# A decoder layer on one core: small products side by side, and another split of the counts in the top-k search

## The chip, the core and the metric

The kernel runs on one core of one Trainium2 chip. TensorE (PE in the rows) multiplies matrices on an array of 128 by 128 and writes to PSUM; VectorE (DVE), ScalarE (ACT) and GpSimd (POOL) work element by element or on small tables; SyncE (SP), ACT and POOL issue DMA transfers. Each engine executes its own queue in a fixed order and waits for others at semaphores. The metric is the device time of one execution in microseconds (us), lower is better.

## What is computed

One layer of a hybrid decoder, for 512 tokens of a prompt and for 8 samples of 4 new tokens with a paged cache of 4096 past tokens each. The width is 1024; everything is float32.

```
x = x + 1/2 * SwiGLU_1(rmsnorm(x))                    # hidden width 2816
gb, gc, hc, q, k, v, qi, ki, wi = split(rmsnorm(x) @ w_in)
y_conv = gb * causal_conv3(gc * hc)                   # 512 channels
I[t, s] = sum_h wi[t, h] * relu(qi[t, h] . ki[s])     # 8 indexer heads of 64
keys = top_k(I over the admissible keys)              # 128 for the prompt, 256 for a sample
attn = softmax(q . k[keys] / 8) @ v[keys]             # 8 heads of 64, 2 key groups
x = x + concat(y_conv, attn) @ w_out
x = x + 1/2 * SwiGLU_2(rmsnorm(x))
```

The new keys, values, indexer keys and convolution states are outputs too.

## The kernel before

The activations stay in SBUF, channels on the partitions, 544 tokens (32 of the samples, 512 of the prompt) in the free dimension. Weights come as float32 through a staging tile `wst` (as many as `WB` of them), and are split in two float32r parts, `whi` by ACT and the rest `wlo` by VectorE or POOL; each product is three matmuls on the parts. The program runs the first feed-forward part, the mixer, and the second feed-forward part.

The mixer is cut in steps that a planner (`PLAN`, `PLAN2`, `LAG`) interleaves; the order of each engine's queue then comes from a scheduler with priorities, at build time. What matters for the change:

- `sample_scores`: for the samples, pages of indexer keys are gathered (`kn`), transposed (`KTp`, then `kt` in SBUF), multiplied with the queries of two samples (`ssc`, two column groups of 64), passed through a relu (`Srel`), and summed over heads (`SC`, four column groups of 32).
- `sample_select`: the exact 256 best of 4100 scores of each query, found by three searches with two bits per round: 8 rounds on the high 16 bits of the score, 8 on the low 16, 7 on the position. A round tests three candidates: it counts the elements at or above each (`flip,cnt`), sums the counts of a query's four partitions by two small transposes (`row`, `col`), compares with the number needed, and forms the next candidates (`cand`). Two counts are VectorE's (L829), one is ACT's with the sign function (L827). The result is `bias`: 0 or a large negative number for each key.
- `prompt_select`: the top 128 of each prompt query, on VectorE, 16 pairs of maximum and replace on `pw` (L941, L942) for each of three blocks.
- `qk`: logits of a quarter of the pages for four samples: four gathers `ckn` by POOL, four `KTp` and `KT` (as many as `KTB` tiles), and eight matmuls `lg`, two for each sample, on the sample's column group of 32. Set 0's raw logits run during the search; set 1's run in `sample_attend`.
- `sample_attend`: adds `bias` to set 0's logits (`lgb`), takes the softmax, then four cycles of values of set 0 (four gathers `cvn`, a transpose `PT`, 32 matmuls `O`) and logits of set 1, then set 1's softmax and four groups of values. Keys and values share four gather buffers. `OT` ends a set.
- `prompt_softmax`: four logits `plg` for each block and head pair, each in a PSUM unit of one bank (`f`, two of them), evicted by VectorE with the mask added. `KTp`, `lg`, `lgb`, `PT` use large units of two banks (`w`, two of them).
- `conv` and `w_out` (`Yo`): matmuls that the planner places between these steps; the second half of `w_out` needs the samples' and the prompt's attention.

In the names of rows, `flip` is also the scratch that the counts write to, and `main` holds constants. A matmul on float32 operands leaves two records.

Of the kernel before, what the change touches and what calls it, by code (L numbers as in the profile page):

```python
# [46 lines left out]
WB = 3  # L47
# [9 lines left out]
LGD = 2  # L57
KTB = 3
# [8 lines left out]
def host_consts():  # L67
# [21 lines left out]
    need = np.where(p % 32 == 2, 2.0 * K_S - 4.0 * SCW, K_S)  # L89
    quarter = 4.0 ** np.arange(8)  # L90
    offs = np.stack([quarter, 2 * quarter, 0.5 - 3 * quarter], axis=1).reshape(1, 24)
    search = np.concatenate([need[:, None], np.broadcast_to([1.0, 1.0, -1.0], (128, 3)), np.broadcast_to(offs, (128, 24))], axis=1)
# [25 lines left out]
class Trunk:  # L118
# [14 lines left out]
    def tp(self, *args):  # L133
        ins = self.nc.tensor.transpose(*args)  # L134
        return self.tc.keep_in_program_order(ins) if self.pin else ins

# [18 lines left out]
    def stream(self, srcs, n, m, kind="", slot=None):  # L155
        """fp32 weights [128, n, m] from DRAM, as the two float32r parts, in the given or the next place of three."""
# [37 lines left out]
    def fmm(self, name, parts, act, n):  # L194
        """two PSUM banks, one per half of the tokens: W^T act over n k-tiles."""
# [35 lines left out]
    def rms(self, ssq):  # L231
        """sums of squares [128 tokens, 5 tiles] -> rn, 1 / root mean square."""
# [19 lines left out]
    def spread(self):  # L252
        """R [128, T]: the row of rn on every partition."""
# [9 lines left out]
    def ffn(self, wg, wu, wd, done, late=False):  # L263
# [3 lines left out]
        def hidden(f, G, U):  # L267
            """G, U: one PSUM tile of equal halves, or (columns, PSUM) pairs."""
# [95 lines left out]
    def begin_units(self):  # L364
        """loads and transposes the activations; the first gate and up units, by halves of the tokens as these come in."""
        nc, tc, i = self.nc, self.tc, self.i
        with tc.tile_pool(name="init", bufs=1) as ip, tc.high_priority(offset=FIRST):
# [13 lines left out]
            def weights(w, n):  # L381
                """w's first 128 columns in n runs of k-tiles: for each a function that loads it, fp32 and the two parts."""
# [57 lines left out]
            def mms(unit, w, hf, order="01234567" * 2):  # L440
                """the high parts of the weights at a k-tile's first mention, the low ones at its second."""
# [112 lines left out]
    def rope(self, v, i, n, nh, kind):  # L554
        """partial rotary on v [n tokens, nh, 64] of token tile i."""
# [32 lines left out]
    def load_half(self, pieces, m, ks=(4, 4), slots=(0, 1)):  # L588
        """w_in columns in runs of ks k-tiles, [128, k, m] each; pieces: (offset in tile, first column, width)."""
# [8 lines left out]
    def later(self, f, depth):  # L598
        """keep f for later; run what lies deeper than depth."""
# [5 lines left out]
    def idx_group(self, g, i, parts, depth=0):  # L605
        """steps; four indexer query heads of token tile i, and for g = 1 the indexer keys and head weights."""
# [45 lines left out]
    def qkv_group(self, g, i, parts, depth=0):  # L652
        """steps; four query heads of token tile i (g: 0, 1), or its keys and values (g: 2)."""
# [45 lines left out]
    def key_transpose(self, kn, name):  # L699
        """eight 128 x 128 transposes of gathered keys, PSUM -> SBUF."""  # L700
# [8 lines left out]
    def sample_scores(self, mp):  # L709
        """indexer scores of the sample queries over all pages: [128 = (bp, jh, b2, rr, t), (jl, p)]."""  # L710
# [20 lines left out]
        def headsum(out, S, bp, jh):  # L731
            self.mm(out, wm[:, bp, jh, :], S, start=True, stop=True)
# [10 lines left out]
        def scores(n):  # L743
            bp = n % 4
            w = self.wunit("ssc")
            for hf in range(2):
                for b2 in range(2):
                    self.mm(w[64 * b2:64 * b2 + 64, hf, :], self.qbi[:, 2 * bp + b2].rearrange("p r t h -> p (r t h)"),
                            kts[n, b2][:, hf * 512:(hf + 1) * 512], start=True, stop=True)
# [4 lines left out]
        def gathered(jh, c):  # L754
            u = self.tunit("SC")
            for bp in range(4):
                headsum(u[32 * bp:32 * bp + 32, :], SS[bp][:, c * 512:(c + 1) * 512], bp, jh)
# [43 lines left out]
    def sample_select(self, mp):  # L801
        """exact top K_S of the 4100 scores of each query (ties: lowest position first) -> bias 0 / -BIG."""
# [16 lines left out]
        def search(src, bits, base0):  # L819
            """[128, 1]: the largest x of base0 to base0 + 2**bits - 1 with K_S elements of the query at or above x,  # L820
            two bits a round: three candidates, counted on the vector engine (two) and the scalar engine."""
            base = mp.tile([128, 1], F32, name="base", tag="base", bufs=3)
            V.memset(base, base0)
            cand = mp.tile([128, 3], F32, name="cand", tag="cand", bufs=2)
            V.scalar_tensor_tensor(cand, self.sgn, base, self.offs[:, bits // 2 - 1], op0=ALU.mult, op1=ALU.add)
            for b in range(bits // 2 - 1, -1, -1):
                nc.scalar.activation(junk2, src, AF.Sign, bias=cand[:, 2:3], accum_out=cnt[:, 2:3])  # L827
                for k in range(2):
                    V.tensor_scalar(junk, src, cand[:, k:k + 1], None, op0=ALU.is_ge, op1=ALU.add, accum_out=cnt[:, k:k + 1])  # L829
                row = mp.tile([128, 32], F32, name="row", tag="row", bufs=2)  # L830
                V.transpose(row, cnt)
                if b:
                    nxt = mp.tile([128, 3], F32, name="nxt", tag="nxt", bufs=2)
                    V.scalar_tensor_tensor(nxt, self.sgn, base, self.offs[:, b - 1], op0=ALU.mult, op1=ALU.add)
# [11 lines left out]
                old, base = base, mp.tile([128, 1], F32, name="base", tag="base", bufs=3)  # L846
                V.tensor_add(base, old, add)
                yield
            return base
# [54 lines left out]
    def prompt_scores(self, pool):  # L904
        """indexer scores of prompt blocks 1..3, causally filled; block 0 keeps every admissible key."""
# [27 lines left out]
    def prompt_select(self, pool, scores):  # L933
        """the top K_P of the scores of each query (ties: lowest position first) -> 0 / -BIG."""
# [13 lines left out]
    def conv(self, cs, pool, early=False):  # L948
        """steps; the gated convolution of the channel chunks cs."""
# [73 lines left out]
    def qk(self, st, q, more):  # L1023
        """PSUM: raw logits of quarter q of the pages, samples 4 st to 4 st + 3; rows (b, g, c, t)."""
        nc = self.nc
        kts, w = [], None

        def logits(b4):
            for rr in range(2):
                self.mm(w[32 * b4:32 * b4 + 32, rr, :], self.qbd[:, 4 * st + b4].rearrange("p g c t -> p (g c t)"),  # L1030
                        kts[b4][:, rr], start=True, stop=not more)

        for b4 in range(4):
# [3 lines left out]
            if b4 >= LGD:  # L1037
                w = w or self.wunit("lg")
                logits(b4 - LGD)
        for b4 in range(4 - LGD, 4):  # L1040
            yield
            w = w or self.wunit("lg")
            logits(b4)
# [19 lines left out]
    def logits_end(self, st, L, mx, ap):  # L1063
        """the logits of the new keys, and the softmax of all."""
# [29 lines left out]
    def pv(self, st, q, L, O, ap):  # L1094
# [9 lines left out]
        for c in range(8):  # L1104
            r = 2 * (c % 4) + c // 4
            for b4 in range(4):
                self.mm(O[32 * b4:32 * b4 + 32, :128], pt[:, c, 32 * b4:32 * b4 + 32],
# [408 lines left out]
```

## Time and profile before

| | us |
|---|---|
| runs shown | 1273.5, 1279.09, 1279.54 |
| median | 1279.09 |
| span of the profiled execution | 1270.2 |
| TensorE, VectorE, ACT, POOL busy | 1230.0, 640.4, 456.4, 209.3 |

The page gives the profiled execution's span, from its first instruction to its last; no time of its own stands beside it, and the runs' times lie 3 to 9 us above it. The span has three parts: the first feed-forward to about 405 us, the mixer to about 861, and the second feed-forward. A window's row gives the busy time of each engine in a stretch, and so tells which is full there. The chain of waits tells in order of time what the end waited for; its pieces are not the whole of an engine's work. Groups by shape give the duration of one instruction.

### The profile page before, as it was taken

To read this page: it belongs to the slowest core of one execution; us is meant where nothing else is said; L and a number is where in the kernel's file an instruction comes from. 1 tells how busy PE (TensorE), PEld (TensorE's weight loads), DVE (VectorE), ACT (ScalarE), POOL (GpSimd) and SP (SyncE) were. 2 spreads that over 40 slices of the span, in tenths; PEclk is the share of its full clock that TensorE was granted. 3 is DMA by queue.
4 is the path that set the end of the run, shared out by engine and by line. 5 is a ranking of instruction groups with operands and counts; after the bars stand their busy time and mean duration, and the time that the engine had idled before them with its cause. 6 is when DMAs were issued, how large, how long until landed. Compare 5 with 4: busy or idle time off the path is not lost.

```text
span 1270.2 us, 22873 instructions
## 1 busy us (share of the span) xinstructions
PE 1230.0 (97%) x9629; PEld 1112.8 (88%) x9629; DVE 640.4 (50%) x1230; ACT 456.4 (36%) x696; POOL 209.3 (16%) x319
## 2 busy tenths in 40 slices
PE   9999999999999999899989989999999999999998
PEld 8999999999999747776667545789999999999998
DVE  5444334433446216999999753265443344433442
ACT  6332122212224464456525556244222122222222
POOL 3200000000000646665413231310000000000000
PEclk9999999999999999999999999999999999999999
DMA  7422332332222553245224443543223323322322
GB/s 231 133 85 84 93 90 84 92 92 84 86 73 69 179 178 106 68 138 169 68 61 140 161 151 124 167 141 113 87 84 93 91 84 87 96 85 84 91 75 74
DMA packets 184363, 136.10 MB, mean 107 GB/s; under 512 B 5706, under 2 KB 172434, under 8 KB 184260
## 3 DMA queue, kind: packets, MB, share of 16 engines
q1 hardware_dynamic: 171700, 91.62, 24.7%
q0 software_dynamic: 11904, 42.26, 10.3%
q8 instruction: 76, 1.25, 0.4%
q10 hardware_dynamic: 656, 0.76, 0.2%
q14 instruction: 27, 0.22, 0.1%
HBM read 131.66 MB, written 2.96 MB: 106 GB/s over the span
## 4 chain that ended last, share of the span: by engine, by line
PE 83%; DVE 10%; DMA 2%; issue 2%; ACT 1%; POOL 1%; DVEq 0%; ACTq 0%; POOLq 0%
PE Y L191 20%; PE U L191 20%; PE G L191 19%; PE Yo L130 4%; DVE flip L829 3%; PE KTp L134 2%; PE lg L130 2%; PE nat L130 2%; DMA ckn<-in_cache_k,ik 2%; PE O L130 2%; PE ssc L130 1%; PE plg L130 1%; PE pO L130 1%; DVE pw L928 1%; PE gc L130 1%
## 5 line engine op out<-in xcount | busy, mean ns | idle before, releaser
L166 ACT ACTIVATE whi<-wst 128x1024 fp32r<-128x1024 f32 (+3 forms) x173 | 172.7, 999 | 582.6 <-PE Y L191 181.2
L171 DVE TENSOR_TENSOR wlo<-wst,whi 128x1024 fp32r<-128x1024 f32 (+3 forms) x156 | 180.7, 1158 | 26.8 <-ACT whi L166 23.1
L191 PE MATMUL Y<-hh,wlo 128*128 128x272 f32 (+2 forms) x704 | 147.6, 288 | 0.0
L191 PE MATMUL Y<-hh,whi 128*128 128x272 f32 (+2 forms) x704 | 147.4, 289 | 0.0
L191 PE MATMUL Y<-hl,whi 128*128 128x272 f32 (+2 forms) x704 | 147.1, 288 | 0.0
L191 PE MATMUL U<-xh,whi 128*128 128x272 f32 x688 | 142.0, 287 | 1.5 <-DVE t L274 1.5
L191 PE MATMUL U<-xh,wlo 128*128 128x272 f32 x688 | 141.6, 288 | 0.0
L191 PE MATMUL U<-xl,whi 128*128 128x272 f32 x688 | 141.3, 287 | 0.0
L191 PE MATMUL G<-xh,whi 128*128 128x272 f32 x656 | 135.6, 287 | 0.0
L191 PE MATMUL G<-xl,whi 128*128 128x272 f32 x656 | 135.0, 287 | 0.0
L191 PE MATMUL G<-xh,wlo 128*128 128x272 f32 x656 | 134.9, 288 | 0.0
L276 DVE TENSOR_TENSOR u<-U,R 128x544 f32<-128x544 f32 x43 | 31.2, 725 | 160.2 <-PE U L191 160.2
L191 PEld LDWEIGHTS Y<-hl,whi 128*128 128x128 f32 x704 | 111.4, 188 | 0.0
L191 PEld LDWEIGHTS Y<-hh,whi 128*128 128x128 f32 x704 | 111.1, 188 | 0.0
L191 PEld LDWEIGHTS Y<-hh,wlo 128*128 128x128 f32 x704 | 110.7, 189 | 0.0
L330 DVE SCALAR_TENSOR_TENSOR x<-Y,x 128x544 f32<-128x544 f32 x46 | 33.3, 725 | 152.2 <-PE Y L191 152.2
L191 PEld LDWEIGHTS U<-xh,whi 128*128 128x128 f32 x688 | 107.1, 188 | 1.6 <-ACT whi L166 1.6
L191 PEld LDWEIGHTS U<-xl,whi 128*128 128x128 f32 x688 | 107.5, 188 | 0.0
L191 PEld LDWEIGHTS U<-xh,wlo 128*128 128x128 f32 x688 | 107.1, 189 | 0.0
L169 POOL TENSOR_TENSOR wlo<-wst,whi 128x1024 fp32r<-128x1024 f32 (+2 forms) x17 | 34.4, 2025 | 423.4 <-ACT whi L166 422.8
L191 PEld LDWEIGHTS G<-xl,whi 128*128 128x128 f32 x656 | 102.6, 188 | 0.0
L191 PEld LDWEIGHTS G<-xh,whi 128*128 128x128 f32 x656 | 102.2, 188 | 0.0
(330 smaller groups left out, 2235.0 us busy)
## 6 DMA issues: line engine op xcount, KB each, us to landing
wst<-in_ffn_w_up SPq DMA_DIRECT2D x44, 512.0 KB, 3.7
wst<-in_ffn_w_gate SPq DMA_DIRECT2D x43, 512.0 KB
wst<-in_ffn_w_down SPq DMA_DIRECT2D x32, 512.0 KB, 4.1
wst<-in_w_in SPq DMA_DIRECT2D x16, 512.0 KB, 4.0
wst<-in_ffn_w_down SPq DMA_DIRECT2D x16, 384.0 KB, 3.5
xn<-in_x_prompt SPq DMA_DIRECT2D x4, 512.0 KB
wst<-in_w_in SPq DMA_DIRECT2D x8, 256.0 KB, 8.9
wst<-in_w_out SPq DMA_DIRECT2D x8, 256.0 KB, 2.6
```

The lines of the kernel that those rows point to most:

```text
L130: ins = self.nc.tensor.matmul(*args, **kw)
L134: ins = self.nc.tensor.transpose(*args)
L166: nc.scalar.activation(hi, st, AF.Copy)
L169: nc.gpsimd.tensor_tensor(lo, st, hi.bitcast(F32), op=ALU.subtract)
L171: nc.vector.tensor_sub(lo, st, hi.bitcast(F32))
L191: self.nc.tensor.matmul(unit[:, i, :c1 - c0], a[:, k, :], b[:, k, c0:c1], start=k == 0 and j == 0, stop=k == n - 1 and j == 2)
L276: nc.vector.tensor_mul(dst.rearrange("p (a b) -> p a b", a=2), src[:, :, :HT], self.R.rearrange("p (a b) -> p a b", a=2))
L330: nc.vector.scalar_tensor_tensor(xc, Y[:, :, :HT], 0.5, xc, op0=ALU.mult, op1=ALU.add)
L829: V.tensor_scalar(junk, src, cand[:, k:k + 1], None, op0=ALU.is_ge, op1=ALU.add, accum_out=cnt[:, k:k + 1])
L928: nc.vector.scalar_tensor_tensor(W, t, wcol, W, op0=ALU.mult, op1=ALU.add)
```

## The change

It has three parts.

1. A new helper `in_a_row` issues a group of matmuls that lie on different parts of the array consecutively, with a raised priority, the one whose operand comes last first. It is used for `ssc`, `SC`, `lg`, `O` and `plg`. In `qk` all eight `lg` now follow the fourth transposes, and `KTB` is 4. In `prompt_softmax` the logits of the two key groups form a pair, which takes one large unit `w` in place of two units `f`. To make room in SBUF, `WB` is 2.
2. In `sample_select` ACT counts two of the three candidates of a round, and VectorE one.
3. The next candidates are formed from the present ones (`nxt = cand + offs`) and not from a base; the base is formed once at the end of each search.

```diff
-WB = 3
+WB = 2
-LGD = 2
-KTB = 3
+KTB = 4
+RUN = 5000
...
-    need = np.where(p % 32 == 2, 2.0 * K_S - 4.0 * SCW, K_S)
+    need = np.where((p % 32 == 1) | (p % 32 == 2), 2.0 * K_S - 4.0 * SCW, K_S)
...
+    def in_a_row(self, last, *others):
+        with self.tc.high_priority(offset=RUN):
+            with self.tc.issue_after(last().ins):
+                for f in others:
+                    f()
...
-            base = mp.tile([128, 1], F32, name="base", tag="base", bufs=3)
-            V.memset(base, base0)
+            top4 = 4.0 ** (bits // 2 - 1)
             cand = mp.tile([128, 3], F32, name="cand", tag="cand", bufs=2)
-            V.scalar_tensor_tensor(cand, self.sgn, base, self.offs[:, bits // 2 - 1], op0=ALU.mult, op1=ALU.add)
+            for k, first in enumerate((base0 + top4, 0.5 - base0 - 2 * top4, 0.5 - base0 - 3 * top4)):
+                V.memset(cand[:, k:k + 1], first)
             for b in range(bits // 2 - 1, -1, -1):
-                nc.scalar.activation(junk2, src, AF.Sign, bias=cand[:, 2:3], accum_out=cnt[:, 2:3])
-                for k in range(2):
-                    V.tensor_scalar(junk, src, cand[:, k:k + 1], None, op0=ALU.is_ge, op1=ALU.add, accum_out=cnt[:, k:k + 1])
+                for k in (1, 2):
+                    nc.scalar.activation(junk2, src, AF.Sign, bias=cand[:, k:k + 1], accum_out=cnt[:, k:k + 1])
+                V.tensor_scalar(junk, src, cand[:, 0:1], None, op0=ALU.is_ge, op1=ALU.add, accum_out=cnt[:, 0:1])
+                if b:
+                    nxt = mp.tile([128, 3], F32, name="nxt", tag="nxt", bufs=2)
+                    V.tensor_add(nxt, cand, self.offs[:, b - 1])
...
-                    V.scalar_tensor_tensor(nxt, self.sgn, base, self.offs[:, b - 1], op0=ALU.mult, op1=ALU.add)
...
-                old, base = base, mp.tile([128, 1], F32, name="base", tag="base", bufs=3)
-                V.tensor_add(base, old, add)
                 yield
+            base = mp.tile([128, 1], F32, name="base", tag="base", bufs=3)
+            V.tensor_scalar(base, cand[:, 0:1], -1.0, add, op0=ALU.add, op1=ALU.add)
...
+        def logits(rr, b4):
+            return lambda: self.mm(w[32 * b4:32 * b4 + 32, rr, :], self.qbd[:, 4 * st + b4].rearrange("p g c t -> p (g c t)"),
+                                   kts[b4][:, rr], start=True, stop=not more)
+        self.in_a_row(*[logits(rr, b4) for rr in range(2) for b4 in (3, 0, 1, 2)])
...
-        for s in (0, 2, 1, 3):
-            g, c = divmod(s, 2)
-            gs = slice(64 * g, 64 * g + 64)
-            w = self.funit("plg")
...
+        for c in range(2):
+            w = self.wunit("plg")
...
+            self.in_a_row(logits(0), logits(1))
```

The order of the queues moves with it. VectorE in the position search: one round before, from the candidates on.

```order
L845 SCALAR_TENSOR_TENSOR cand<-main,add,nxt 128x3
L847 TENSOR_TENSOR base<-base,add 128x1
L829 TENSOR_SCALAR flip,cnt<-low,cand 128x1056
L834 SCALAR_TENSOR_TENSOR nxt<-main,base 128x3
L829 TENSOR_SCALAR flip,cnt<-low,cand 128x1056
L831 STREAM_TRANSPOSE row<-cnt 128x32
L836 TENSOR_REDUCE tot<-row 128x8
L922 TENSOR_SCALAR pw_4231<-rel,wis 128x384
L838 TENSOR_SCALAR step<-tot,main 128x32
L985 TENSOR_TENSOR gc<-gc,R_5071 128x272
L153 COPY kTs<-kT 128x32
```

The same engine and search after.

```order
L840 TENSOR_SCALAR flip,cnt<-low,cand 128x1056
L843 TENSOR_TENSOR nxt<-cand,main 128x3
L1023 TENSOR_TENSOR yc_7099<-gb,yc_7099 128x272 x2
L953 MATCH_REPLACE pw_4230<-m_7433,pw_4230 128x256
L952 MAX m_7436<-pw_4230 128x8
L953 MATCH_REPLACE pw_4230<-m_7436,pw_4230 128x256
L845 STREAM_TRANSPOSE row<-cnt 128x32
L952 MAX m_7439<-pw_4230 128x8
L847 TENSOR_REDUCE tot<-row 128x8
L953 MATCH_REPLACE pw_4230<-m_7439,pw_4230 128x256
L849 TENSOR_SCALAR step<-tot,main 128x32
```

One count of the round is gone, and maximum and replace of the prompt's selection (`pw`) stand between the round's small operations.

ACT during the search on the low half, before: `KT` evicts transposed keys, `L` logits.

```order
L827 ACTIVATE flip,cnt<-low,cand 128x1056
L706 ACTIVATE KT<-KTp 128x1024
L827 ACTIVATE flip,cnt<-low,cand 128x1056
L672 ACTIVATE nq<-nat,rn 128x128
L673 ACTIVATE vn<-nat,rn 128x128
L706 ACTIVATE KT<-KTp 128x1024
L827 ACTIVATE flip,cnt<-low,cand 128x1056
L1061 ACTIVATE L_6481<-lg 128x1024
L827 ACTIVATE flip,cnt<-low,cand 128x1056
```

ACT in the same search after: `qTs` and `nq` belong to the queries and keys of the prompt.

```order
L839 ACTIVATE flip,cnt<-low,cand 128x1056
L161 ACTIVATE qTs<-qT 128x2x128
L839 ACTIVATE flip,cnt<-low,cand 128x1056
L716 ACTIVATE KT<-KTp 128x1024 x2
L839 ACTIVATE flip,cnt<-low,cand 128x1056
L623 ACTIVATE nq<-nat,rn 128x256
L161 ACTIVATE qTs<-qT 128x2x128
L839 ACTIVATE flip,cnt<-low,cand 128x1056
L716 ACTIVATE KT<-KTp 128x1024
```

Two counts belong to each round now, and evictions and normalizations stand between them.

TensorE in `sample_attend`, in the first cycle of set 1's logits, before (`pPT` and `pO` belong to the prompt's values).

```order
L134 MATMUL KTp<-main,ckn 128x128 x16
L130 MATMUL plg<-kTs,qTs 128x384 x2
L130 MATMUL lg<-KT,qbd 32x512 x6
L134 MATMUL KTp<-main,ckn 128x128 x8
L130 MATMUL plg<-kTs,qTs 128x384
L134 MATMUL pPT<-main,P 128x128 x4
L130 MATMUL lg<-KT,qbd 32x512 x2
```

The end of the same cycle after; its four `KTp` stand further ahead.

```order
L132 MATMUL plg<-kTs,qTs 128x384 x2
L136 MATMUL pPT<-main,P 128x128 x8
L132 MATMUL pO<-pPTs,vn 64x256 x2
L136 MATMUL pPT<-main,P 128x128 x8
L132 MATMUL pO<-pPTs,vn 64x256 x4
L132 MATMUL plg<-kTs,qTs 128x256 x2
L132 MATMUL pO<-pPTs,vn 64x256 x2
L132 MATMUL plg<-kTs,qTs 128x256 x2
L132 MATMUL lg<-KT,qbd 32x512 x8
```

The eight `lg` stand together, behind three pairs of `plg` and the prompt's transposes and values.

## Rows read from the trace of the kernel before

**Rows 1.** The page's first part: busy time, share of the span, instructions.
```profile
PE 1230.0 (97%) x9629; PEld 1112.8 (88%) x9629; DVE 640.4 (50%) x1230; ACT 456.4 (36%) x696; POOL 209.3 (16%) x319
```

**Rows 2.** Windows: from:to, length, then busy us of each engine, clock, DMA.
```profile
487.10:538.50 51.40, 43.29 (x333) 40.87 (x331) 48.58 (x131) 25.01 (x44) 34.45 (x61) 0.93 0.24 71
538.50:585.00 46.50, 44.98 (x293) 30.29 (x292) 44.33 (x113) 28.59 (x43) 30.31 (x46) 1.00 0.46 142
585.00:651.00 66.00, 59.93 (x396) 45.66 (x397) 62.94 (x176) 33.19 (x61) 25.40 (x45) 1.00 0.32 90
651.00:760.00 109.00, 98.67 (x822) 68.65 (x820) 85.63 (x251) 51.51 (x101) 32.41 (x36) 0.98 0.43 139
```

**Rows 3.** Tiles `bias` and `OT`: durations min/median/max in ns, first and last start.
```profile
L870 DVE TENSOR_SCALAR bias<-low,base x1: 486/486/486, 651.3 to 651.3; 128x1056 bf16<-128x1056 uint16 x1
...
  DMA half<-in_c_half: 2.2, 1
...
L134 PE MATMUL OT<-main,On x2: 328/328/328, 777.1 to 836.6; 128*128 128x128 f32 x2
```

**Rows 4.** The chain, 650 to 840 us: start, length, what (a count is of records).
```profile
657.20 4.74 PE hc L130 x24
...
680.67 2.01 PE O L130 x64
...
684.19 0.95 POOL ckn L695
...
685.44 6.27 DMA ckn<-in_cache_k,ik
...
756.45 2.01 PE O L130 x64
...
834.04 2.12 PE O L130 x60
```

**Rows 5.** The chain at side-by-side groups and at single ones.
```profile
463.74 0.99 PE SC L130 x8
...
466.92 0.98 PE SC L130 x2
...
596.93 1.83 PE lg L130 x4
...
692.91 0.85 PE plg L130 x4
...
697.23 0.84 PE plg L130 x2
```

**Rows 6.** Groups by shape on TensorE, 405 to 880 us: busy, mean ns | idle.
```profile
L130 PE MATMUL lg<-KT,qbd 128*32 128x512 f32 x128 | 40.9, 598 | 0.0
```

**Rows 7.** Groups by shape on ACT, 480 to 660 us.
```profile
L827 ACT ACTIVATE flip<-low,cand 128x1056 bf16<-128x1056 uint16 x15 | 17.6, 1174 | 14.8 <-DVE base L847 10.1 <-DVE cand L845 3.5 <-DVE low L854 1.1
L706 ACT ACTIVATE KT<-KTp 128x1024 f32<-128x1024 f32 x16 | 16.0, 1019 | 12.3 <-PE KTp L134 7.5 <-DVE low L853 4.7
```

**Rows 8.** The page's last part: DMA issues, KB each, median us to landing.
```profile
wst<-in_w_in SPq DMA_DIRECT2D x8, 256.0 KB, 8.9
```

**Rows 9.** VectorE: groups by shape, 480 to 660 us, then lines L941 and L942.
```profile
L829 DVE TENSOR_SCALAR_CACHE_REDUCE flip<-low,cand 128x1056 uint16<-128x1056 uint16 x30 | 39.2, 1307 | 0.0
...
L847 DVE TENSOR_TENSOR base<-base,add 128x1 f32<-128x1 f32 x23 | 5.7, 248 | 0.0
...
L829 DVE DVE_READ_ACCUMULATOR flip<-low,cand 128x1 f32 x30 | 2.5, 82 | 0.0
...
L941 DVE MAX8 m<-pw x48: 409/552/696, 620.6 to 738.2; 128x8 f32<-128x384 f32 x16, 128x8 f32<-128x256 f32 x16, 128x8 f32<-128x512 f32 x16
...
L942 DVE MATCH_REPLACE8 pw<-m,pw x48: 396/542/685, 622.9 to 740.5; 128x384 f32<-128x384 f32 x16, 128x256 f32<-128x256 f32 x16, 128x512 f32<-128x512 f32 x16
```

**Rows 10.** Windows of 25 us, columns as in rows 2.
```profile
625.00:650.00 25.00, 19.46 (x128) 14.92 (x127) 25.00 (x59) 10.38 (x19) 9.02 (x11) 1.00 0.25 69
650.00:675.00 25.00, 20.06 (x146) 18.50 (x145) 24.65 (x62) 10.93 (x15) 5.77 (x6) 0.93 0.23 64
```

More of the change, by code (lines that the diff above doesn't have):

```diff
@@ L731, in headsum @@
         def headsum(out, S, bp, jh):
-            self.mm(out, wm[:, bp, jh, :], S, start=True, stop=True)
+            return self.mm(out, wm[:, bp, jh, :], S, start=True, stop=True)
         sc = self.sc
@@ L745, in scores, with part @@
             w = self.wunit("ssc")
[L746 to L749, printed above, removed]
+            def part(hf, b2):
+                return lambda: self.mm(w[64 * b2:64 * b2 + 64, hf, :], self.qbi[:, 2 * bp + b2].rearrange("p r t h -> p (r t h)"),
+                                       kts[n, b2][:, hf * 512:(hf + 1) * 512], start=True, stop=True)
+            self.in_a_row(*[part(hf, b2) for hf in range(2) for b2 in (1, 0)])
             S = self.lgt(n % 4, "Srel")
@@ L755, in gathered @@
             u = self.tunit("SC")
-            for bp in range(4):
-                headsum(u[32 * bp:32 * bp + 32, :], SS[bp][:, c * 512:(c + 1) * 512], bp, jh)
+            self.in_a_row(*[lambda bp=bp: headsum(u[32 * bp:32 * bp + 32, :], SS[bp][:, c * 512:(c + 1) * 512], bp, jh)
+                            for bp in (3, 0, 1, 2)])
             dst = sc[:, 512 * c:512 * c + 512]
@@ L1025, in qk @@
         nc = self.nc
[L1026 to L1031, printed above, removed]
+        kts = []
         for b4 in range(4):
@@ L1036, in qk @@
             yield
[L1037 to L1043, printed above, removed]
+        yield
+        w = self.wunit("lg")
+        def logits(rr, b4):
+            return lambda: self.mm(w[32 * b4:32 * b4 + 32, rr, :], self.qbd[:, 4 * st + b4].rearrange("p g c t -> p (g c t)"),
+                                   kts[b4][:, rr], start=True, stop=not more)
+        self.in_a_row(*[logits(rr, b4) for rr in range(2) for b4 in (3, 0, 1, 2)])
+        yield
         return w
@@ L1103, in pv, with part @@
         nc.scalar.activation(pt.rearrange("p a b -> p (a b)"), wf, AF.Copy)
-        for c in range(8):
+        def part(c, b4):
             r = 2 * (c % 4) + c // 4
-            for b4 in range(4):
-                self.mm(O[32 * b4:32 * b4 + 32, :128], pt[:, c, 32 * b4:32 * b4 + 32],
-                                 vs[b4][:, r * 128:(r + 1) * 128], start=False, stop=q == 3 and c == 7)
+            return lambda: self.mm(O[32 * b4:32 * b4 + 32, :128], pt[:, c, 32 * b4:32 * b4 + 32],
+                                   vs[b4][:, r * 128:(r + 1) * 128], start=False, stop=q == 3 and c == 7)
+        self.in_a_row(*[part(c, b4) for c in range(8) for b4 in (3, 0, 1, 2)])
     def pv_end(self, st, O, rs, ap):
@@ L1162, in prompt_softmax, with logits @@
         mx = ap.tile([128, 4], F32, name="pmx", tag="pmx", bufs=2)
-        for s in (0, 2, 1, 3):
-            g, c = divmod(s, 2)
-            gs = slice(64 * g, 64 * g + 64)
-            w = self.funit("plg")
-            self.mm(w[:, :N], self.qT[gs, 2 * ch + c, q0:q0 + 128], self.kT[gs, NS:NS + N], start=True, stop=True)
-            nc.vector.tensor_tensor_reduce(P[:, s, :N], w[:, :N], self.pw[j], 0.125, -3.0e38, op0=ALU.add, op1=ALU.max,
-                                           accum_out=mx[:, s:s + 1])
+        for c in range(2):
+            w = self.wunit("plg")
+            def logits(g):
+                gs = slice(64 * g, 64 * g + 64)
+                return lambda: self.mm(w[:, g, :N], self.qT[gs, 2 * ch + c, q0:q0 + 128], self.kT[gs, NS:NS + N], start=True, stop=True)
+            self.in_a_row(logits(0), logits(1))
+            for g in range(2):
+                s = 2 * g + c
+                nc.vector.tensor_tensor_reduce(P[:, s, :N], w[:, g, :N], self.pw[j], 0.125, -3.0e38, op0=ALU.add, op1=ALU.max,
+                                               accum_out=mx[:, s:s + 1])
         nm = ap.tile([128, 4], F32, name="pnm", tag="pnm", bufs=2)
```

8 lines of the change are left out of this document (4 added, 4 removed).

## Prediction

> **What bounds the kernel now.** I read the page first, then the windows, then the chain, then groups by shape. TensorE is busy 97% of the span [rows 1], but that share is an average. The two feed-forward parts, before about 405 and after about 861 us, are back-to-back matmuls and the change touches neither, so everything is decided in the mixer between. There the windows [rows 2] show two regimes. From 487.1 us, where the scores are complete, until the selection's `bias` at 651.3 [rows 3], VectorE is the full engine: 48.6 of 51.4 us in the search on the high half, 44.3 of 46.5 in the next, 62.9 of 66.0 in the last. Behind `bias` VectorE is no longer full, and the chain alternates between gathers of the cache and short TensorE groups: the first `O` group of values at 680.67, the fourth at 756.45, the last one at 834.04 [rows 4], with `OT` at 836.6 [rows 3]. So the end of the mixer is when `bias` comes, plus a chain of gathers.
>
> **Side-by-side groups.** A head sum alone takes 0.98 us, four in a row 0.99; two logit matmuls on one column group take 1.83; a `plg` pair side by side takes 0.85, and one alone 0.84 [rows 5]. (A piece counts records, two for each of these matmuls.) All of `lg` is busy 40.9 us [rows 6]. Eight matmuls in a row on four column groups are two passes of 0.98, so the eight groups of eight are 8 x 1.96 = 15.7 and the saving is up to 25 us of TensorE; the 16 head sums fall from about ten pieces of 0.98 to four, -6; `plg` saves half of what stood alone, -5. Of these 36 us only the head sums lie on the path: they stand in the chain ahead of the search. I credit -6 there and nothing for `lg` and `plg`, since TensorE waits in those stretches anyway: 59.9 of 66.0 and 98.7 of 109.0 [rows 2]. If all 25 of `lg` counted, the sum would come out 25 lower. Evicting a unit of that size costs ACT 1.02 us [rows 7], more than half of the 1.96 that its eight matmuls would take, and that cost stays. The Trainium skill, "TensorEngine Tiling (Array Packing)", section "PSUM Bottleneck", says the same in general: tiling speeds up TensorE and leaves the emptying of PSUM as it was.
>
> **Buffers.** Two staging tiles instead of three make the third part of the first `w_in` block wait for a release; its load of 256 KB has a median of 8.9 us to landing [rows 8]. Against the cover that the other two parts give I take +2 us (0 to +9). The fourth key buffer lets the fourth transposes go ahead of the logits, worth up to the 1.83 of a pair per cycle. The search therefore begins at 487 - 6 + 2 = 483.
>
> **The selection, phase by phase.** In each of 23 rounds VectorE loses one count and its read (1.31 us, and 0.08 for the read) and the base add (0.25) [rows 9]: 23 x 1.64 = 38 us less. But the order of instructions shows that the place is filled: of the 48 pairs of maximum and replace (0.55 and 0.54 us in the median [rows 9]) that pick the prompt's keys, 8 stand ahead of `bias` before and 35 after. That is +27 x 1.1 = +30 us, and pieces of the convolution and weight splits moved ahead of `bias` add about 13. Summed over the order with durations from this trace, VectorE's work between the scores and `bias` is 167 us before (163 measured) and 174 after. VectorE does not come free; it does other work earlier.
> ACT gains a count per round, 1.17 + 0.19 us [rows 7]. Its two counts do not stand together: between them the order has key evictions (1.02 each), logit evictions and weight conversions. So I take for each round the larger of VectorE's row sum and ACT's.
> High half: 42, with some 3 us where the two alternate, 45 (before 51). Low half: 52 (before 46.5), as ACT is busy 28.6 us in that stretch already [rows 2] and most of this stands ahead of or between the counts. Position search with what prepares it, again VectorE's own: 66.0 - 7 x 1.64 + 30 + 11 = 95. Together 192, so `bias` at 483 + 192 = 675 to 677, about 25 us later than now. The lower end is VectorE never waiting, 483 + 174 = 657. The upper end is 690: half of the rounds losing one more key eviction and conversion, 12 x 1.1.
>
> **From `bias` to the end of attention.** Now 680.67 - 651.3 = 29.4 us pass to the first `O`, with TensorE working on convolution (five pieces of the chain, the first 4.74 us [rows 4]; they come to 17 us) and with a wait of 2.2 for the table `half` [rows 3]. These pieces stand ahead of `bias` after. What is left is the bias product, four 1.2 us additions, exponentials and two transposes: 19 us. First `O` at 696, +15.
> Three cycles of gathers to the fourth `O` take 25.3 us each now (756.45 - 680.67 over three). The chain shows a gather's landing as 6.27 us, and the issue before it as 1.25 us earlier [rows 4]; four stand behind one another. With the fourth transposes no longer delayed I would give 22.5. Against this, the softmax pairs now use the two large PSUM units, which `KTp`, `lg`, `PT` need too, and they wait for VectorE, which begins this stage with the rest of the prompt's selection (13 pairs and the masks, some 20 us). I take 24.5: fourth `O` at 769.5, +13. From there to the end of attention it is 80 us now (756.45 to 836.6), a wait for the last logits and four rounds of value gathers that TensorE hardly holds up; I take 79.5. So 849 against 836.6. `w_out` and the second feed-forward follow as before. With half a microsecond at the start of the kernel, the sum is **+13 us** on the span of 1270.2, or 1283. The median of the runs shown, 1279.09, lies 9 above the span; on it I predict **1292**.
>
> **Rivals.**
> A, faster: VectorE never waits for ACT. `bias` at 657, first `O` at 676, cycles 22.5, last set 78: end of attention at 821.5, -15 on a span of 1270; with the cycles at their best, -22. Time 1257 to 1264. For it: ACT is busy only 25.0 of 51.4, 28.6 of 46.5 and 33.2 of 66.0 [rows 2], so there is room. Against it: counts stand behind evictions in a fixed order, and an engine can be half idle and late.
> B, no change: half of ACT's waits vanish, `bias` 666, first `O` 685, cycles 24, last set 79.5: 836.5, so 1279.
> C, much slower, decided by the PSUM units: if each cycle's logits wait behind two more pairs of softmax, because a unit comes free only when VectorE has evicted it, cycles become 28, the first `O` 705 with `bias` at 686, the last set 82: 871, +34, so 1313. It decides where the softmax pairs stand ahead of the logits in TensorE's order, which they do in the first cycle. The Trainium skill, "TensorEngine Tiling (Array Packing)", "Gotcha 1: PSUM Pressure", warns that row tiles need different banks; here that is the pair's second bank.
> D, the clock: in the last set TensorE has no filler left (`w_out`'s first half is used up by then), so it stands idle for most of 4 x 14 us. The granted clock was 0.93 from 650 to 675, where TensorE was busy 20.1 of 25 us, but 1.00 from 625 to 650 at 19.5 [rows 10]. Were the 22 us of `w_out` that follow run at half clock for a quarter of their length, that is +6 on the forecast. The Trainium skill, "TensorE: Matmul & The Clock Gate", "HAM oscillation", speaks against such a tail: gaps in which TensorE waits for DMA lower its clock. The rows here bear it out only in part, so it gets no place in the sum; it is inside the forecast's range.
>
> **How the numbers follow.** Forecast (+6 to +24, 1285 to 1303) 0.44, with D among it; A 0.30; B 0.18; C 0.08. The likeliest gives 1292. The range keeps 8 in 10: it cuts the best third of A and the worst of C, 1259 to 1311. A difference below 0.5% (6.4 us) is about what a measurement of this kernel can't tell from none. Faster is A, 0.30; same is B, 0.18; slower is the forecast and C, 0.52.
>
> **What would show it.** Right: in the profile after, VectorE is full between the scores and `bias`, with rows of maximum and replace inside the position search; `bias` near 676; the four early `O` groups at most 25 us apart; TensorE idle between the last four. Wrong: ACT's counts back to back and `bias` before 660 (A); cycles of 28 us with `lg` or `KTp` waiting for `plg`'s eviction (C); or a search that begins later than 487, which would mean that two staging tiles hold up the mixer's start.

## The result

The kernel after takes 1320.99 us (median; 1319.79 to 1324.13), against 1278.38 us for the kernel before in the same runs: 1.0334 times as long, 95% interval 1.0306 to 1.0363. The forecast was 1292 with a range to 1311, so the sign was right and the size was not: +42.6 us and not +13. The two profiles below lie further apart, 52.1 us in span: the one of the kernel before is of one of its shortest executions (1270.2 us, where 39 later ones have 1270.8 to 1281.7), and the one after is of the longest of its four, so some 9 us between the two are not the change's.

The two profiles, at the points that the prediction named (all in us from the start of the span; the columns of the experiments are told of below):

| | before | after | forecast for after | e4 | e7 | e11 |
|---|---|---|---|---|---|---|
| scores complete, search begins | 487.2 | 497.4 | 483 | 497.8 | 496.5 | 479.7 |
| `bias` | 651.3 | 684.3 | 676 | 684.0 | 654.2 | 635.2 |
| first `O` group | 680.7 | 703.0 | 696 | 707.5 | 679.5 | 655.3 |
| second `O` group | 705.8 | 756.7 | 720.5 | 727.5 | 708.8 | 676.3 |
| fourth `O` group | 756.4 | 811.7 | 769.5 | 772.0 | 753.7 | 722.7 |
| last `OT` | 836.6 | 888.0 | 849 | 850.1 | 829.4 | 800.6 |
| span | 1270.2 | 1322.3 | 1283 | 1285.0 | 1263.0 | 1239.4 |

The page of the kernel after, its busy times and the row of the granted TensorE clock in 40 slices (tenths of full speed), which answer to [rows 1]:

```profile
PE 1209.1 (91%) x9629; PEld 1117.6 (85%) x9629; DVE 609.2 (46%) x1167; ACT 480.7 (36%) x742; POOL 206.7 (16%) x319
...
PEclk9999999999999989999976999669999999999999
```

TensorE lost 21 us of busy time and 6 points of its share. The granted clock fell in five slices of the mixer: to 8 tenths at 463 to 496 us, to 7 and 6 at 661 to 727, and to 6 at 826 to 893. Before, all 40 slices have a 9, which is 90% or more.

The windows of the kernel after: the three phases of the search, as in [rows 2], then `bias` to the first `O`, the first cycle, and the last set of values (the columns are those of [rows 2]):

```profile
497.40:549.40 52.00, 47.83 (x383) 43.72 (x383) 40.26 (x109) 36.42 (x63) 39.80 (x66) 0.97 0.25 74
549.40:608.20 58.80, 53.75 (x415) 41.84 (x412) 42.58 (x128) 46.71 (x81) 35.13 (x58) 1.00 0.52 167
608.20:684.30 76.10, 57.77 (x412) 52.22 (x413) 75.64 (x227) 36.26 (x60) 21.99 (x37) 0.95 0.23 65
684.30:703.00 18.70, 7.05 (x34) 3.11 (x33) 17.30 (x43) 7.25 (x12) 0.00 (x0) 0.50 0.00 0
703.00:756.70 53.70, 43.63 (x314) 27.62 (x314) 33.09 (x116) 32.03 (x88) 7.71 (x8) 0.87 0.27 85
836.00:888.00 52.00, 18.85 (x297) 16.29 (x297) 0.60 (x3) 8.56 (x15) 11.22 (x12) 0.64 0.37 122
```

The three phases last 52.0, 58.8 and 76.1 us, 187 together where they lasted 164. VectorE is full in the last one alone, 75.6 of 76.1 us; the prediction expected it full in all three. In the first two (497.4 to 608.2 us) VectorE waits for ACT: the transpose of a round's counts (`row`) had to wait for ACT's counts (us, times; there are 16 rounds),

```profile
  ACT flip L839: 15.7, 12
```

and no such wait stands in these two phases before. The first cycle of gathers takes 53.7 us, and no engine is full in it. In the last set TensorE is busy 18.9 of 52 us.

When the search begins, and what the mixer's loads made others wait for between 395 and 500 us (times in ns, then first and last start; for the wait: us, times):

```profile
L819 DVE TENSOR_SCALAR flip<-sc x1: 885/885/885, 497.4 to 497.4; 128x1056 int32<-128x1056 int32 x1
```

```profile
  DMA wst<-in_w_in: 19.8, 4
```

ACT waits twice, 9.8 us together, and TensorE once, 4.9 us, which is counted a second time for its weight load. Before, no wait for a load of `w_in` stands in that stretch. `bias`, and the maxima of the prompt's selection (L952, L941 before) that started between the scores and `bias`:

```profile
L881 DVE TENSOR_SCALAR bias<-low,base x1: 477/477/477, 684.3 to 684.3; 128x1056 bf16<-128x1056 uint16 x1
```

```profile
L952 DVE MAX8 m<-pw x35: 381/543/690, 603.1 to 683.7; 128x8 f32<-128x384 f32 x16, 128x8 f32<-128x256 f32 x16, 128x8 f32<-128x512 f32 x3
```

35 of 48 ran ahead of `bias`, and the 0.55 us of [rows 9] holds. The chain around the `O` groups, which answers to [rows 4]:

```profile
703.01 3.76 PE O L132 x64
706.92 4.62 DMA ckn<-in_cache_k,ik
...
756.75 2.49 PE O L132 x64
...
786.49 1.88 PE O L132 x64
```

```profile
811.75 1.88 PE O L132 x64
...
843.72 2.36 PE O L132 x72
...
883.89 3.67 PE O L132 x64
...
890.33 14.03 PE Yo L132 x95
```

From the first group to the second there are 53.7 us, and then 29.7 and 25.3. TensorE's groups inside that first cycle (busy, mean ns | idle before them and what ended it):

```profile
L132 PE MATMUL plg<-kTs,qTs 64*128 64x128 f32 (+3 forms) x60 | 13.5, 541 | 0.5 <-DVE L L1149 0.5
...
L132 PE MATMUL pO<-pPTs,vn 128*64 128x256 f32 x40 | 6.1, 400 | 1.6 <-ACT pPTs L1203 1.6
L136 PE MATMUL pPT<-main,P 128*128 128x128 f32 x40 | 5.7, 282 | 0.0
...
L132 PE MATMUL O<-cvn,PTs 128*32 128x128 f32 x74 | 4.2, 402 | 3.2 <-ACT PTs L1109 3.2
L132 PE MATMUL lg<-KT,qbd 128*32 128x512 f32 x16 | 1.9, 598 | 0.0
```

60 of the 64 records of `plg`, 40 of the 80 `pPT` and 40 of the 80 `pO` records are in this one cycle; the logits `lg`, for which the cycle exists, take 1.9 us, as estimated from [rows 5]. They start at 739.9 us, 36.9 behind the first `O` group, where before it was 13.0. The chain between the two groups ends in the prompt's softmax, with ACT's exponentials (`P`); only behind them comes ACT's eviction `PTs`, which released the second group:

```profile
738.91 2.51 ACT P L1185 x8
...
743.94 1.13 PE plg L132 x4
...
750.75 2.81 ACT P L1185 x8
...
753.82 1.97 ACT P L1185 x8
755.78 0.92 ACT PTs L1109
```

### The profile page after: what moved, and what is told of

It is laid out like the page before. It is cut to its first block, busy times and chain, and to the rows that moved or that the text cites. A ratio compares the mean times of both kernels' runs of the same rounds, so it can differ in the third digit from the quotient of the medians.

```text
span 1322.3 us, 22857 instructions
## 1 busy us (share of the span) xinstructions
PE 1209.1 (91%) x9629; PEld 1117.6 (85%) x9629; DVE 609.2 (46%) x1167; ACT 480.7 (36%) x742; POOL 206.7 (16%) x319
## 4 chain that ended last, share of the span: by engine, by line
PE 78%; DVE 9%; DMA 5%; ACT 5%; issue 2%; POOL 1%; SPq 0%; ACTq 0%; DVEq 0%; POOLq 0%
PE Y L201 20%; PE U L201 19%; PE G L201 19%; PE Yo L132 4%; PE nat L132 4%; PE KTp L136 2%; PE O L132 2%; DMA cvn<-in_cache_v,ik 1%; DMA wst<-in_w_in 1%; DVE pw L953 1%; PE lg L132 1%; DVE m L952 1%; DMA ckn<-in_cache_k,ik 1%; DVE flip L840 1%; DVE pw L939 1%
## 5 line engine op out<-in xcount | busy, mean ns | idle before, releaser
L286 DVE TENSOR_TENSOR u<-U,R 128x544 f32<-128x544 f32 x43 | 31.1, 724 | 160.8 <-PE U L201 160.8
L201 PEld LDWEIGHTS G<-xh,wlo 128*128 128x128 f32 x656 | 102.2, 189 | 0.0
```

The costliest lines, as they stand in the source:

```text
L286: nc.vector.tensor_mul(dst.rearrange("p (a b) -> p a b", a=2), src[:, :, :HT], self.R.rearrange("p (a b) -> p a b", a=2))
```

## The experiments

The theory formed from the two traces was that three things each cost time of their own: two staging tiles delay the mixer's loads; VectorE, given time by the new counts, is filled with the prompt's selection ahead of `bias`, and ACT's queue holds the counts up; and the softmax pairs in the large PSUM units stand in front of the first cycle's logits. The rival was the clock: the groups leave TensorE idle, its clock falls, and everything is longer for that. The times below are medians, and the kernel before stood at 1276 to 1279 beside them.

**One part alone.** Two staging tiles in the kernel before.

```diff
-WB = 3
+WB = 2
```

> The kernel before, with two staging tiles in place of three and nothing else. Three-causes theory (staging, selection and softmax pairs each cost time of their own): loads of w_in wait for a tile, the search begins 8 to 12 us later than in the kernel before (at 495 to 499 against 487.2), and the time is 1284 to 1292. Clock theory (the grouped matmuls leave TensorE idle, its clock falls, and that is the loss): no group is formed here, so 1275 to 1282, with the search at 487 to 489.

Measured: 1295.41, ratio 1.0111 (1.0064 to 1.0158). The search begins here:

```profile
L808 DVE TENSOR_SCALAR flip<-sc x1: 709/709/709, 501.1 to 501.1; 128x1056 int32<-128x1056 int32 x1
```

That is 13.9 us later than before, with no other edit, and waits for loads of `w_in` stand there as in the kernel after (21.9 us in four; none before). So the wait is the expected one; the delay and the time are both a little above their ranges.

The new counts and candidates in the kernel before.

```diff
-                nc.scalar.activation(junk2, src, AF.Sign, bias=cand[:, 2:3], accum_out=cnt[:, 2:3])
-                for k in range(2):
-                    V.tensor_scalar(junk, src, cand[:, k:k + 1], None, op0=ALU.is_ge, op1=ALU.add, accum_out=cnt[:, k:k + 1])
+                for k in (1, 2):
+                    nc.scalar.activation(junk2, src, AF.Sign, bias=cand[:, k:k + 1], accum_out=cnt[:, k:k + 1])
+                V.tensor_scalar(junk, src, cand[:, 0:1], None, op0=ALU.is_ge, op1=ALU.add, accum_out=cnt[:, 0:1])
...
```

> The kernel before, with the new counts and candidates of the samples' search and nothing else. In this order 24 of the 48 pairs of maximum and replace stand ahead of the bias, 8 before. Three-causes theory: from the scores to the bias 175 to 187 us in place of 164, the first group of values up to 10 us later, the time 1280 to 1295. Clock theory: the search forms no group, so 1272 to 1282.

Measured: 1311.70, ratio 1.0253 (1.0214 to 1.0292), above the ranges of both theories. From the scores to `bias` it took 194 us, 7 above the upper end, and the first group of values came at 707.5, 27 us later than before and not up to 10.

The softmax pairs in the kernel before.

```diff
-        for s in (0, 2, 1, 3):
...
-            w = self.funit("plg")
...
+        for c in range(2):
+            w = self.wunit("plg")
...
+            self.in_a_row(logits(0), logits(1))
```

> The kernel before, with the prompt's logits as pairs in one large PSUM unit and nothing else. The order now has 32 plg and 40 pPT in the first cycle of the samples' logits, 4 and 4 before. Three-causes theory: first to second group of values 45 to 55 us in place of 25.2, later cycles no longer than now, the time 1295 to 1308. Clock theory: TensorE does less work in a pair, but as only 5 us of it goes, the clock stays near 0.99 and the time within 1274 to 1284.

Measured: 1328.16, ratio 1.0383 (1.0342 to 1.0423): this part alone costs at least as much as the whole change, and more than either theory expected. The first cycle lasted 64.0 us, and the next two 32.1 and 30.5. The clock theory expected no loss in any of these three runs, two of which form no group at all, and falls with them.

**One part taken out.** The kernel after with `plg` one by one in the small units again, the reverse of the last diff.

> The kernel after, with the prompt's logits one by one in small units again. Three-causes theory: first to second group of values at most 30 us in place of 53.7, the time 1290 to 1303. Clock theory: all other groups stay, the clock stays near 0.956, and the time is above 1312.

Measured: 1284.93, ratio to the kernel before 1.0059 (1.0030 to 1.0088). 36 of the 42.6 us are gone. The chain's `O` groups:

```profile
707.46 1.88 PE O L132 x64
...
727.50 1.88 PE O L132 x64
...
750.48 2.00 PE O L132 x64
...
772.02 1.95 PE O L132 x64
```

The cycles are 20.0, 23.0 and 21.5 us, shorter than the 25.3 of before: without the pairs, the logits in a row and the fourth key buffer are worth 11 us over three cycles, as far as the order of this run goes, where most of the prompt's selection stands ahead of `bias`. The clock was 0.973 in this run, and the search still began at 497.8 and `bias` came at 684.0.

The kernel after with the search's counts as before, the reverse of the second diff.

> The kernel after, with the search's counts and candidates as before (two counts on VectorE, a base). If the new counts cost time inside this kernel too (187 us from the scores to the bias, 164 before): 165 to 172 us, the time 1298 to 1310; the first cycle of the samples' logits stays at 45 to 64 us, since the softmax pairs are still in the large units. If the counts cost nothing once the pairs fill the first cycle: above 1316.

Measured: 1309.12, ratio 1.0258 (1.0225 to 1.0290). From the scores to `bias` 164.8 us, just under the range, and the first cycle 53.8. So the new counts cost some 12 us inside this kernel (10 by the ratios), and the long first cycle does not depend on them.

The kernel after with three staging tiles; for the space, with three key buffers and the logits `lg` in the order of before.

```diff
-WB = 2
+WB = 3
-KTB = 4
+KTB = 3
+LGD = 2
```

> The kernel after, with three staging tiles, and with the logits in the order and with the three key buffers of before, which the space asks for. If two staging tiles cost 10 us at the mixer's start: the search begins at 484 to 491 in place of 497.4, and the time is 1306 to 1318; the cycles of gathers are not shorter than in the kernel after. If the later start is a matter of order and not of staging: the search still begins at 495 to 500.

Measured: 1332.95, ratio 1.0427 (1.0386 to 1.0467), slower than the kernel after and above what was expected. But the search begins early:

```profile
L820 DVE TENSOR_SCALAR flip<-sc x1: 1197/1197/1197, 479.8 to 479.8; 128x1056 int32<-128x1056 int32 x1
```

479.8 is 17.6 us earlier than in the kernel after, so staging accounts for the whole delay of the start. It is also 7.4 earlier than before. The gain was lost again behind it: 194.5 us to `bias`, and cycles of 61.1, 34.1 and 31.1 us. Which of the three edits did that can't be told from this run. In its first two phases, 122.5 us in place of 110.8, TensorE is busy 119 us; e2_select, with the same key buffers and order of `lg`, also has 122.5 there, and the cause of that is open.

The kernel after with `plg` one by one, without a raised priority, but each in a large unit.

```diff
-            w = self.funit("plg")
+            w = self.wunit("plg")[:, 0, :]
```

(against e4_after_f)

> The kernel after, with the prompt's logits one by one, no pair and no raised priority, but each in a large PSUM unit. Order theory (the two large units are handed out in the program's order, so the softmax stands in the first cycle): 29 plg and 40 pPT in the first cycle as with pairs, first to second group of values 45 to 64 us, the time 1312 to 1340. If the cost came from the pairs standing side by side or from their priority: at most 35 us, and the time below 1300.

Measured: 1329.50, ratio 1.0420 (1.0392 to 1.0448). The chain's `O` groups:

```profile
703.86 3.76 PE O L132 x64
...
764.25 1.95 PE O L132 x64
...
796.41 1.96 PE O L132 x64
```

The first cycle is 60.4 us with nothing side by side. Pairing and priority are not the cause; the unit is. In the order of the instructions 29 `plg` and 40 `pPT` stand in the first cycle here, 30 and 40 in the kernel after, and 4 and 4 in the kernel before. The order was made when the kernel was built, so it shows where they stand, and this run shows what it costs.

**What stands ahead of `bias`.** As e4_after_f, with each maximum of the prompt's selection held behind `bias`.

```diff
-        V.tensor_scalar(self.bias, low, X, -BIG, op0=ALU.is_lt, op1=ALU.mult)
+        self.bias_ins = V.tensor_scalar(self.bias, low, X, -BIG, op0=ALU.is_lt, op1=ALU.mult).ins
...
-                nc.vector.max(m8, W)
+                with self.tc.issue_after(self.bias_ins):
+                    nc.vector.max(m8, W)
                 nc.vector.match_replace(W, m8, W, TAKEN)
...
-                after = dict(B="A", Q="A", I="B", V="S", K="Q", L="S", P="IK", c="Ie", e="AS")
+                after = dict(D="V", B="A", Q="A", I="B", V="S", K="Q", L="S", P="IK", c="Ie", e="AS")
```

> As e4_after_f (no softmax pairs), with each maximum of the prompt's selection held behind the bias, so that none of the 48 pairs stands ahead of it in VectorE's order (35 there). If the bias is late because VectorE is filled with this selection: 155 to 165 us from the scores to the bias in place of 186, the time 1265 to 1282. If it is late because ACT's two counts wait behind other work in ACT's order: still 178 to 187, and the time above 1285, as 48 pairs then stand behind the bias.

Measured: 1263.11, ratio 0.9888 (0.9853 to 0.9924), 1.1% faster than the kernel before. All 48 maxima now start behind `bias` (654.2 us):

```profile
L953 DVE MAX8 m<-pw x48: 410/555/696, 654.6 to 750.9; 128x8 f32<-128x384 f32 x16, 128x8 f32<-128x256 f32 x16, 128x8 f32<-128x512 f32 x16
```

The three phases of its search (columns of [rows 2]):

```profile
496.50:548.40 51.90, 46.58 (x383) 42.35 (x382) 40.16 (x109) 36.43 (x63) 39.84 (x66) 1.00 0.25 74
548.40:603.90 55.50, 50.72 (x392) 39.39 (x390) 41.90 (x116) 45.75 (x79) 33.98 (x54) 1.00 0.55 176
603.90:654.20 50.30, 45.93 (x321) 40.41 (x320) 46.81 (x119) 33.38 (x58) 22.32 (x36) 0.97 0.28 79
```

158 us in place of 186 in e4_after_f, and nearly all of it in the last phase: 50.3 us, where e4_after_f has 75.6. So VectorE's filling is what made that phase long. The price is paid in part behind `bias`: the first cycle is 29.2 us here and 20.0 there.

As e4_after_f, with the search of before.

> As e4_after_f (no softmax pairs), with the search as before: what is left of the change is the samples' groups in a row, four key buffers and two staging tiles. If the new counts cost 20 us of the bias: the bias at 663 to 670 in place of 684, the time 1266 to 1280, level with the kernel before, since the shorter cycles pay for the staging. If the selection moved ahead of the bias is worth as much behind it as it costs ahead: 1282 to 1290.

Measured: 1277.46, ratio 0.9999 (0.9985 to 1.0014). `bias` came at 661.4, 1.6 us earlier than expected; the time is in the range. The shorter cycles pay for the staging, as forecast for this run, and no more.

As e7_dafter, with the search of before.

> As e7_dafter (no softmax pairs, the prompt's selection held behind the bias), with the search's counts as before. If the new counts are worth something once VectorE is kept free for them: from the scores to the bias 160 to 170 us in place of 157.7, and the time 1266 to 1280 against 1263. If ACT's waits eat the gain: 155 to 158, and the time within 1258 to 1265.

Measured: 1274.99, ratio 1.0000 (0.9982 to 1.0018). The time is as expected if the new counts are worth something, but the reason given for it is wrong. The three phases:

```profile
495.50:547.90 52.40, 43.17 (x314) 40.80 (x312) 49.57 (x131) 22.84 (x40) 35.01 (x59) 0.87 0.24 71
547.90:594.20 46.30, 42.11 (x323) 34.51 (x322) 43.61 (x119) 30.33 (x46) 28.29 (x48) 0.96 0.49 153
594.20:640.60 46.40, 41.05 (x258) 28.34 (x256) 44.98 (x126) 27.16 (x55) 16.23 (x27) 0.96 0.26 77
```

145 us, 12.6 less than in e7_dafter with the new counts. In the second phase ACT is busy 45.8 of 55.5 us with two counts a round and 30.3 of 46.3 with one. So with VectorE kept free the new counts lengthen the search. What makes e10_oldsel_dafter slower in the end lies behind `bias`: 33.2 us to the first `O` in place of 25.3, as convolution work stands there, and 35.9 from `OT` to the second feed-forward in place of 25.0. `OT` itself still comes 3.2 us earlier, but 193 records of `w_out` (24.55 us) stand in one piece behind it in place of 95 (12.99 us). Which of this is due to the counts and which to the order they bring about is open. Against e8_oldsel_f, which differs by the held selection alone, the search is 20 us shorter (145 and 165) and the time the same within 0.2%: a `bias` that comes earlier is not yet a gain in time.

The kernel after, pairs and all, with the prompt's selection held behind `bias`.

> The kernel after with the prompt's selection held behind the bias and nothing else; the softmax pairs stay in the large units. If the bias and the first cycle are separate causes: the bias at 650 to 660 as in e7_dafter, but first to second group of values 55 us or more, as the softmax there now also waits for the whole selection; the time 1305 to 1335. If the first cycle was long only because the bias was late: at most 35 us and below 1285.

Measured: 1317.99, ratio 1.0320 (1.0286 to 1.0354).

```profile
L881 DVE TENSOR_SCALAR bias<-low,base x1: 489/489/489, 654.1 to 654.1; 128x1056 bf16<-128x1056 uint16 x1
```

```profile
676.81 3.76 PE O L132 x64
...
755.62 1.95 PE O L132 x64
...
781.38 1.88 PE O L132 x64
```

`bias` is 30 us earlier than in the kernel after, and the second `O` group comes at 755.6 and not at 756.7. The first cycle took up the whole gain. With the softmax in front, the second group waits for the prompt's selection and softmax, whenever `bias` comes: in this cycle `plg` alone waits 14.4 us for VectorE.

**Both remedies.** As e7_dafter, with three staging tiles; one buffer fewer each for the queries' rows and the prompt's relu makes the space.

```diff
-WB = 2
+WB = 3
-NQB = 4
+NQB = 3
...
-                    t = pool.tile([128, 512], F32, name="rel", tag="rel", bufs=2)[:, :N]
+                    t = pool.tile([128, 512], F32, name="rel", tag="rel", bufs=1)[:, :N]
```

> As e7_dafter, with three staging tiles; the space comes from one fewer buffer for the queries' rows and for the prompt's relu. Staging theory: the search begins at 480 to 488 in place of 496.5, and the time is 1249 to 1258, clearly below the kernel before. If the smaller buffers cost as much in the search: 1258 to 1270.

Measured: 1241.16, ratio 0.9724 (0.9689 to 0.9760), below both kernels and below what was expected. Its busy times, the start of its search and its `bias`:

```profile
PE 1196.7 (97%) x9624; PEld 1109.0 (89%) x9629; DVE 617.4 (50%) x1167; ACT 482.1 (39%) x742; POOL 211.6 (17%) x319
```

```profile
L819 DVE TENSOR_SCALAR flip<-sc x1: 1202/1202/1202, 479.7 to 479.7; 128x1056 int32<-128x1056 int32 x1
L820 DVE TENSOR_TENSOR flip<-sc,flip x1: 1258/1258/1258, 481.0 to 481.0; 128x1056 int32<-128x1056 int32 x1
...
L881 DVE TENSOR_SCALAR bias<-low,base x1: 488/488/488, 635.2 to 635.2; 128x1056 bf16<-128x1056 uint16 x1
```

TensorE is back at 97% of a span that is 31 us shorter than before. The search begins 16.8 us earlier than in e7_dafter, and `bias` 19.0.

## Why the prediction was right and wrong

- **The head sums in a row**: right as far as the runs go. Credited 6 us; with three staging tiles the search begins at 479.7 and 479.8 with the new groups (e11_dafter_wb3, e6_after_wb3) and at 487.2 to 488.7 without (the kernel before, e2_select, e3_plg), 7 to 9 us. No run changes the head sums alone.
- **Two staging tiles**: the step that failed first. Taken at +2 with 9 as the upper end, from one load's landing time; it costs 13.9 alone and 17.6 in the kernel after. The row [rows 8] prices one load. A tile has to come free for every load, and in the trace after ACT waits twice for `w_in`, 9.8 us together, and TensorE once, 4.9. The sign of being wrong that the prediction named, a search that begins later than 487, came true.
- **The search**: right in its sum, and partly by luck. Forecast 192, measured 187; by phase 45, 52 and 95 were forecast, and 52.0, 58.8 and 76.1 measured: two are 7 too low and one 19 too high. That VectorE's freed time is filled was shown by holding that work back (e7_dafter, 28 us, 25 of them in the last phase). The first two phases were mis-sized: each round was priced at the longer engine's sum, but there `row` waits for ACT in 12 of 16 rounds, 15.7 us. ACT's two counts take 2 x (1.17 + 0.19) = 2.7 us, and VectorE's two took 2 x (1.31 + 0.08) = 2.8: the count moved to the other engine, and the longer side stayed as long. The second count on ACT costs 12.6 us with VectorE kept free (e10_oldsel_dafter). The forecast's reason, other work between ACT's two counts, is a small part: in the mean 3.1 and 3.2 us pass in these phases from the start of the first to the end of the second, where the two alone take 2.7. The sum of VectorE's work over the order, 167 and 174 us, is also above the windows, 156 before and 158 after.
- **From `bias` to the first `O`**: right. 19 forecast, 18.7 measured, without the wait for `half`.
- **The cycles**: the step that failed by most. 73.5 us forecast for three, 108.7 measured. The mechanism stood in rival C, which it gave 0.08: the large units. It was priced as two more pairs in each cycle, 28 us. Measured, nearly all the softmax stood in the first cycle, and against the kernel before this cost 28.5 us there and 4 in the next. The order of the instructions had shown four `KTp` and then the pairs ahead of `lg`, and I read its end and did not count: 30 of 32 `plg` in one cycle. With the units of before the cycles are 21.5 us in the mean (e4_after_f), better than the forecast's 24.5 and its best of 22.5, and 24.7 where the selection stands behind `bias` (e7_dafter).
- **The last set**: 79.5 forecast, 76.2 measured; right.
- **The clock (rival D)**: its condition came true and its price did not. The granted clock was 0.64 in the last set, where TensorE stood idle. The first piece of `w_out` behind it took 14.03 us where the same 95 records took 12.98 before, +1 and not +6. In the first cycle the clock of 0.87 means that at most 14 of 53.7 us ran at the lower level, which could cost 7 of the 28.5 us at most. The lower clock comes with the waits: e4_after_f has 0.973 and is 36 us faster, and e11_dafter_wb3 has 0.987 with all groups but the `plg` pairs. e7_dafter has 0.982 and is faster than the kernel before at 0.99. What the clock costs over the whole mixer was not measured by itself.
- **The sum**: against the forecast's 849 for the end of attention, the start is 14.4 later, the search 6 shorter, the first `O` another 1, the cycles 35 longer, the last set 3 shorter; together 39, as measured (888), with `bias` taken at the forecast's 676. In time it is 29 and not 39: the forecast put the median 9 above the span, and after, the median lies 1.3 below the profile's span. That term was read from a profile of one of the shortest executions before. The parts are not additive between kernels: by their ratios, the pairs alone cost 49 us, the counts alone 32, the staging alone 14, and all three with the logits in a row 43. A delay of `bias` is hidden where the first cycle is bound by the softmax, as e12_dafter_pairs shows.

That the three together explain the loss rests on e4_after_f, e7_dafter and e11_dafter_wb3: with the units, the selection's place and the staging mended in turn, the time goes 1321, 1285, 1263, 1241. The last is 35 us below the kernel before: small units and three staging tiles are its own, but the held selection is new, and was not tried on it alone. Whether the new counts would pay in a queue of ACT without the evictions between them was not tried either; two counts alone would still take 2.7 us there.

## What to carry to other kernels

A buffer that two streams of work take in turn is also an order: before a tile is moved to another pool, count what the pool's other users then wait for, and count it stretch by stretch in the new order of the instructions. Time that is taken off a full engine goes to whatever is ready, and that need not be what the path waits for; hold the rest back explicitly and then measure the gain in time, not only at the point it was meant for. Work moved to another engine pays only if the longer of the two sums gets shorter; here it went from 2.8 to 2.7 us. And a buffer given up for space is priced by how often it must come free, not by one transfer.

## What the runs showed of the hardware

- Eight float32 `lg` matmuls on four column groups of 32 took 1.9 us, where two on one column group took 1.83 [rows 5]: the four groups ran side by side at nearly full gain.
- With TensorE busy 18.9 of 52 us the granted clock was 0.64, and an `O` group of 32 matmuls took 3.7 us in place of 1.9, the two levels of 1.2 and 2.4 GHz. From `bias` to the first `O`, with TensorE busy 7.1 of 18.7 us, it was 0.50. From its first group of values to `OT` the last set took 44.0 us all the same, and 44.4 before; in the kernel after its `O` groups waited 28.3 us for gathers.
